# Modulation group 10: from four column products on TensorE to four row sums on VectorE

## The chip, the cores and the metric

The kernel runs on one core of a Trainium2 chip. Its time is the device time of one execution in microseconds (us), and a kernel's figure is the median over its runs. Five engines work in parallel, each through its own instructions in order: TensorE (PE, matrix products; PEld is its weight load), VectorE (DVE, elementwise arithmetic), ScalarE (ACT, activations, copies and casts), GpSimd (POOL, nearly unused here) and SyncE (SP), which issues nearly all DMA transfers from main memory (HBM) into the on-chip memory (SBUF). Products are collected in PSUM banks and taken from there by VectorE or ScalarE.

## The reference

One decoder layer over 256 tokens of width 2048, in float32. What matters here:

```python
mod = jax.nn.silu(c) @ w_ada[l] + b_ada[l]          # c: (1, 2048), w_ada: (2048, 12288)
shift_m, scale_m, gate_m, shift_f, scale_f, gate_f = jnp.split(mod[:, None, :], 6, axis=-1)
h = rms_norm(x, norm_mix_g[l]) * (1.0 + scale_m) + shift_m
proj = h @ w_in[l]                                   # attention heads | Mamba-2 heads
mix = jnp.concatenate([attn, ssm], axis=-1) @ w_out[l]
x = x + gate_m * mix
h = rms_norm(x, norm_ffn_g[l]) * (1.0 + scale_f) + shift_f
x = x + gate_f * conv_ffn(h, w_up[l], ...)           # then a last RMSNorm
```

`mod` is a vector of 12,288 numbers made from one vector `c`; its weights are 96 MB, 96 blocks of 128 outputs. Blocks 40 to 43 are part of `gate_m`, with which the output projection is scaled.

## The kernel before, in words

**Matrix products.** A large product (`w_in`, `w_out`, `w_up`, `w_down`) comes in units of 1 MB. A unit is loaded by SP into a staging buffer (`load_unit`, L250), split by `hi_lo_part` (L255) into a rounded half `h_...` (cast on ACT, L258) and a remainder `l_...` (subtraction on DVE, L259), 1024 columns at a time, and then multiplied by `mm3` (L276 to L279): three products for each block, two with the rounded half and one with the remainder. So no unit's products can all run before DVE has made its remainders. From the step `open` to the step `close2` there are three staging buffers, used in turn by the units of the large products and of the modulation alike: the load of a unit waits until the unit three before it has been used up.

**The modulation.** The 96 blocks of `mod` are 24 groups of four, and each group is four 1 MB units. There are two ways of working a unit, and the set `ON_PE` (L39) says for each group which one (`ada_unit`, L206). A group in `ON_PE`: a unit holds four of the 16 slices of the long axis for all four blocks, and PE multiplies each slice with its part of silu(c) (L217), four products of 32 columns that go to four quarters of one PSUM bank; after the fourth unit ACT copies the bank (`row`, L221), four one-column products turn it into columns (`adc`, L224) and DVE copies these into `mod` (L227). A group not in `ON_PE`: a unit holds one block, transposed, and a single DVE instruction multiplies it with silu(c) along the free axis and sums it up into one column of `mod` (L210), 2048 elements in each of 128 rows, followed by the read of its accumulator. The layout of `w_ada` is made on the host for either way; the bytes are the same.

**The order.** The first part of the kernel (projection, attention, state-space heads, output projection) follows a list written by hand, `ORDER` (L70). Its names: `ada.g.i` is unit i of modulation group g; Q, B, Z, V are units of the input projection; S0, S1, S2 are the stages of an attention head; `an`, `cb` and `dt` prepare the norm and the state-space heads; T1, T2, N, NG are the stages of these heads; O.0.i and O.1.i are units of the output projection. Around group 10 it reads:

```python
S1.5 S2.3 S0.7 ada.10.0 S2.4 ada.10.1 Q4.3 S1.6 dt S1.7 S2.5 ada.10.2 B3.1 ada.10.3 B3.2 ada.11.0 ada.11.1 S2.6
Z3.0 CS.0.8 S2.7 an ada.11.2 CS.8.12 Z3.1 cb.0 cb.1 ZS T1.0 T1.1 ada.11.3 O.0.0 ada.12.0 T2.0 T1.2 N.0 T2.1
```

From this list a planner with a cost model of its own makes one fixed instruction order for each engine; some steps (`HPS`, L32, the head stages among them) get a higher priority there. An instruction whose input is late holds up all that stand behind it on its engine.

**The steps that matter here.** B3.0, B3.1, B3.2 end with a convolution of each result (`conv_pair`, L359): DVE adds up `u` (L398), ACT starts the sum (L365), and DVE adds three shifted terms to it (L367). Z3.1 is the last unit of the input projection; DVE adds its result into `sz` (L388), and then ACT takes silu of `sz` (L373, step ZS) and of `cxs` (L370, CS.8.12). T1.0, the first state-space step, starts on PE with the transpose `xt` of `cxs` (L533). The gate from group 10 is first read at L638, ahead of the first output unit's scaling.

Of the kernel before, what the change touches and what calls it, by code (L numbers as in the profile page):

```python
# [35 lines left out]
          + [[32 + 4 * g + i for i in range(4)] for g in range(4)]  # L36
          + [[48 + 2 * g, 64 + 2 * g, 49 + 2 * g, 65 + 2 * g] for g in range(8)]
          + [[80 + 4 * g + i for i in range(4)] for g in range(4)])
ON_PE = {0, 6, 9, 10, 11, 12, 13, 14, 16}  # L39

HEADS = [(h, 8 + h) for h in range(8)]
XS = [(24 + 2 * i, 25 + 2 * i) for i in range(4)]
# [52 lines left out]
def hymba_layer(ctx, tc, xT, c_row, cT, w_ada, vecs, consts, relb, onehot, w_vdt, w_in, w_out, w_up1, w_up, w_dn, outT):  # L95
# [103 lines left out]
    def ada_load(g, i):  # L199
        ws = ws_tile(f"ada{g}_{i}")  # L200
        nc.sync.dma_start(ws[:, :D], w_ada[4 * g + i])
        return ws
# [3 lines left out]
    def ada_unit(g, i):  # L206
        ws = ada_pre.pop((g, i)) if (g, i) in ada_pre else ada_load(g, i)
        if g not in ON_PE:
            j = GROUPS[g][i]
# [458 lines left out]
    def ada_step(g, i):  # L668
        ada_unit(g, i)
        if g < 8:  # L670
            if g in ON_PE:
                if i == 3:
# [198 lines left out]
def _layout(a):  # L871
# [22 lines left out]
    for g, t in enumerate(GROUPS):  # L894
        for i in range(4):
            if g in ON_PE:
                ada.append(np.stack([wa[4 * i:4 * i + 4, :, c, :] for c in t], axis=2)
# [37 lines left out]
```

## Time and profile before

| | us |
|---|---|
| median of 3 runs | 1192.63 (1192.25 to 1193.84) |
| the profiled execution | 1191.71 |
| its span, first to last instruction | 1189.9 |
| busy: PE, PEld, DVE, ACT | 1162.5, 1112.3, 914.0, 637.7 |

The profile is one execution, and all positions below are us from the start of its span. The span is 1.81 us shorter than that execution's device time, and that execution was 0.92 us shorter than the median. A row of the timeline gives start, duration, engine, line, operation, output and inputs, shape and count, and in brackets the idle time before it with what ended it. The group of work around `ada.10` lies between 258 and 303, of the whole hand-ordered part (0 to about 460).

### The profile page before, as it was taken

Reading aid. Unit: us, or ns where it says so; the run is one execution under the profiler, and the core shown is the slowest. Engines: PE = TensorE matmul, PEld = TensorE weight load, DVE = VectorE, ACT = ScalarE, POOL = GpSimd, SP = SyncE. Lnnn points to the kernel's source line nnn. Section 1 sums busy time; section 2 is a strip of 40 time slices with the busy share of each in tenths; the row PEclk is TensorE's granted clock in tenths of the full one; section 3 lists DMA queues with packets and bytes.
Section 4 is the critical chain, followed back from the end, with each engine's and each line's share of the span. In section 5 each row is a group of like instructions: output and inputs, shape, how many; then the busy total and the mean of one; then the engine's idle time right before and its main releaser. Section 6 shows DMA issues by size and latency. Waiting matters only on the chain.

```text
span 1189.9 us, 23403 instructions
## 1 busy us (share of the span) xinstructions
PE 1162.5 (98%) x9760; PEld 1112.3 (93%) x9760; DVE 914.0 (77%) x1380; ACT 637.7 (54%) x959; POOL 0.9 (0%) x7
## 2 busy tenths in 40 slices
PE   7899999999999999999999999999999999999996
PEld 3899999988888898999999999999999999999995
DVE  3999969977988899786699974446898888655554
ACT  5545434357786545545576754444555555555552
POOL 0000000000000000000000000000000000000000
PEclk8899999999999999999999999999999999999998
DMA  9989898777766997987555435558878776545552
GB/s 369 414 307 360 322 346 313 252 277 254 284 245 215 367 384 292 366 318 288 201 190 196 162 116 192 193 193 283 298 288 313 285 279 218 202 147 195 195 195 96
DMA packets 47444, 309.60 MB, mean 260 GB/s; under 512 B 5568, under 2 KB 6761, under 8 KB 16105
## 3 DMA queue, kind: packets, MB, share of 16 engines
q1 hardware_dynamic: 46170, 307.04, 70.3%
q10 hardware_dynamic: 1168, 1.06, 0.5%
q8 instruction: 76, 1.25, 0.4%
q14 instruction: 30, 0.25, 0.1%
HBM read 305.98 MB, written 2.11 MB: 259 GB/s over the span
## 4 chain that ended last, share of the span: by engine, by line
PE 86%; DVE 6%; DMA 5%; ACT 1%; issue 1%; SPq 0%; DVEq 0%; ACTq 0%
PE ua L279 7%; PE da L278 7%; PE da L277 7%; PE ua L278 7%; PE da L279 7%; PE ua L277 7%; PE u1a L277 3%; PE u2a L278 3%; PE u1a L278 3%; PE u2a L277 3%; PE wa L277 3%; PE u1a L279 3%; PE u2a L279 3%; PE va L348 3%; PE wa L279 3%; PE wa L278 3%
## 5 line engine op out<-in xcount | busy, mean ns | idle before, releaser
L258 ACT CAST h_u<-s_u 128x1024 fp32r<-128x1024 f32 x176 | 184.8, 1051 | 196.6 <-PE ua L278 94.6
L259 DVE TENSOR_TENSOR l_u<-s_u,h_u 128x1024 fp32r<-128x1024 f32 x176 | 214.2, 1222 | 65.1 <-ACT h_u L258 64.6
L277 PE MATMUL ua<-h,h_u 128*128 128x256 f32 x704 | 194.3, 276 | 0.0
L278 PE MATMUL ua<-h,h_u 128*128 128x256 f32 x704 | 194.3, 276 | 0.0
L279 PE MATMUL ua<-h,l_u 128*128 128x256 f32 x704 | 194.3, 276 | 0.0
L279 PE MATMUL da<-g,l_d 128*128 128x256 f32 x704 | 194.3, 276 | 0.0
L278 PE MATMUL da<-g,h_d 128*128 128x256 f32 x704 | 194.3, 276 | 0.0
L277 PE MATMUL da<-g,h_d 128*128 128x256 f32 x704 | 194.1, 276 | 0.0
L259 DVE TENSOR_TENSOR l_d<-s_d,h_d 128x1024 fp32r<-128x1024 f32 (+1 forms) x128 | 108.8, 887 | 83.6 <-ACT h_d L258 83.6
L277 PE MATMUL wa<-hT,h_w 128*128 128x256 f32 x576 | 163.9, 285 | 4.6 <-ACT h_w L258 3.5
L278 PE MATMUL wa<-hT,h_w 128*128 128x256 f32 x576 | 161.0, 280 | 0.0
L279 PE MATMUL wa<-hT,l_w 128*128 128x256 f32 x576 | 160.1, 280 | 0.4 <-DVE l_w L259 0.4
L258 ACT CAST h_d<-s_d 128x1024 fp32r<-128x1024 f32 (+1 forms) x128 | 98.2, 782 | 114.9 <-PE da L278 106.8
L210 DVE SCALAR_TENSOR_TENSOR ada<-ada,cb 128x2048 f32<-128x2048 f32 x60 | 136.9, 2284 | 11.0 <-DMA ada<-w_ada 10.9
L278 PEld LDWEIGHTS da<-g,h_d 128*128 128x128 f32 x704 | 132.1, 188 | 0.0
L277 PEld LDWEIGHTS ua<-h,h_u 128*128 128x128 f32 x704 | 132.1, 188 | 0.0
L278 PEld LDWEIGHTS ua<-h,h_u 128*128 128x128 f32 x704 | 132.1, 188 | 0.0
L279 PEld LDWEIGHTS ua<-h,l_u 128*128 128x128 f32 x704 | 132.1, 188 | 0.0
L279 PEld LDWEIGHTS da<-g,l_d 128*128 128x128 f32 x704 | 132.1, 188 | 0.0
L277 PEld LDWEIGHTS da<-g,h_d 128*128 128x128 f32 x704 | 132.1, 188 | 0.0
L277 PEld LDWEIGHTS wa<-hT,h_w 128*128 128x128 f32 x576 | 109.4, 190 | 12.9 <-ACT h_w L258 4.6
L258 ACT CAST h_w<-s_w 128x1024 fp32r<-128x1024 f32 x72 | 73.7, 1048 | 88.9 <-PE wa L278 47.3
(237 smaller groups left out, 2676.9 us busy)
## 6 DMA issues: line engine op xcount, KB each, us to landing
ada<-w_ada SPq DMA_DIRECT2D x96, 1024.0 KB, 6.9
s_u<-w_up SPq DMA_DIRECT2D x88, 1024.0 KB, 5.0
s_d<-w_dn SPq DMA_DIRECT2D x64, 704.0 KB, 4.0
s_w<-w_in SPq DMA_DIRECT2D x36, 1024.0 KB, 7.5
s_o<-w_out SPq DMA_DIRECT2D x16, 1024.0 KB, 6.5
s_v<-w_vdt SPq DMA_DIRECT2D x8, 1040.0 KB, 8.8
x<-xT SPq DMA_DIRECT2D x4, 512.0 KB, 4.8
outT<-x SPq DMA_DIRECT2D x2, 640.0 KB, 3.0
```

The costliest lines, as they stand in the source:

```text
L210: dve.scalar_tensor_tensor(ws[:, :D], ws[:, :D], 1.0, cb, op0=ALU.mult, op1=ALU.mult, accum_out=mod[:, j:j + 1])
L258: act.copy(wh[:, :m], ws[:, o:o + m])
L259: dve.tensor_sub(wl[:, :m], ws[:, o:o + m], wh[:, :m].bitcast(F32))
L277: pe.matmul(o, whs, a[:, 0:T], start=first, stop=False)
L278: pe.matmul(o, whs, a[:, T:2 * T], start=False, stop=False)
L279: pe.matmul(o, wls, a[:, 0:T], start=False, stop=last)
L348: pe.matmul(va[tt][i][:, :n], lo if st == 1 else hi, (wl if st == 2 else wh)[:, s], start=f and st == 0, stop=l and st == 2)
```

## The change

Group 10 is taken out of `ON_PE`. Its four units stay at their places in `ORDER` and are loaded as before, in the other layout. The four groups of products (L217), the copy on ACT (L221), the one-column products (L224) and the copy into `mod` (L227) go; four instructions of L210, each with its accumulator read, come. One PSUM tile of the tag `ada` and one of `aux` fewer are handed out.

```diff
-ON_PE = {0, 6, 9, 10, 11, 12, 13, 14, 16}
+ON_PE = {0, 6, 9, 11, 12, 13, 14, 16}
```

## Rows read from the trace of the kernel before

**Rows 1.** Busy time by stretch: PE, PEld, DVE, ACT, POOL, clock, DMA share, GB/s.

```profile
120.00:140.00 20.00, 20.00 (x179) 20.00 (x178) 20.00 (x28) 7.85 (x9) 0.00 (x0) 1.00 0.91 336
262.00:277.10 15.10, 15.10 (x118) 12.92 (x117) 6.90 (x15) 9.62 (x25) 0.00 (x0) 1.00 0.74 267
277.10:328.70 51.60, 51.60 (x411) 43.00 (x410) 47.08 (x99) 40.50 (x82) 0.00 (x0) 1.00 0.74 277
332.50:402.50 70.00, 69.83 (x556) 57.92 (x556) 59.81 (x125) 47.58 (x95) 0.00 (x0) 1.00 0.65 238
```

**Rows 2.** Chain of waits, 270 to 302: start, time on the chain, what.

```profile
270.23 0.99 PE adp L217 x6
...
278.96 1.83 PE adp L217 x10
...
289.23 0.99 PE adp L217 x8
...
294.48 0.99 PE adp L217 x8
295.47 0.32 PE wa L279
295.79 0.12 PE wa L277
...
300.91 0.12 PE adc L224 x2
...
301.41 0.56 PE adc L224 x6
```

**Rows 3.** Timeline of DVE, 30 to 33: one unit of a row group.

```profile
30.23 2.28 DVE L210 SCALAR_TENSOR_TENSOR ada<-ada,cb 128x2048 f32<-128x2048 f32 x1
32.44 0.08 DVE L210 DVE_READ_ACCUMULATOR ada<-ada,cb 128x1 f32 x1
```

**Rows 4.** Timeline of DVE, 271 to 320: holes, and the copy into `mod`.

```profile
274.38 0.69 DVE L398 TENSOR_TENSOR u<-cxs,wa 128x512 f32<-128x512 f32 x1 [2.40 <-PE wa L279]
277.11 1.23 DVE L259 TENSOR_TENSOR l_w<-s_w,h_w 128x1024 fp32r<-128x1024 f32 x1 [2.05 <-ACT h_w L258]
...
299.33 1.37 DVE L367 SCALAR_TENSOR_TENSOR cxs<-u,vec,cxs 128x255 f32<-128x255 f32 x3 [0.76 <-ACT cxs L365]
...
302.53 0.16 DVE L227 COPY mod<-adc 128x4 f32<-128x4 f32 x1
...
311.01 1.37 DVE L367 SCALAR_TENSOR_TENSOR cxs<-u,vec,cxs 128x255 f32<-128x255 f32 x3 [0.67 <-ACT cxs L365]
```

**Rows 5.** Timeline of SP's queue: loads of `ada.10.0` and `10.1`, `10.2`, B3.1, `10.3`.

```profile
258.91 8.51 SPq L201 DMA_DIRECT2D ada<-w_ada  x2
...
279.96 0.33 SPq L201 DMA_DIRECT2D ada<-w_ada  x1
280.38 0.38 SPq L252 DMA_DIRECT2D s_w<-w_in  x1
280.86 0.38 SPq L201 DMA_DIRECT2D ada<-w_ada  x1
```

**Rows 6.** Chain of waits, 308 to 333.

```profile
308.40 6.82 DMA s_w<-w_in
...
319.05 1.75 DVE rs_attn L300
...
328.72 0.80 ACT sz L373
...
330.55 1.90 ACT cxs L370
...
332.50 0.44 PE xt L533 x2
```

**Rows 7.** Landing of the `ada` load issued at 258.91, and of all issued from 255 to 300.

```profile
ada<-w_ada SPq DMA_DIRECT2D x1, 1024.0 KB, 9.3
...
DMA to landing us min/median/max: 4.8/6.8/9.3
```

## The prediction

> **What bounds the kernel now.** Read the busy times by stretch first [rows 1]. From 262 to 328.7 PE is busy in every microsecond, with no idle time the profile shows, at a granted clock of 1.00. DVE stands at 6.90 of 15.10 us up to 277.1, and then at 47.08 of 51.60 us: 91%, with 4.52 us of holes. After the first state-space step has started, from 332.5 to 402.5, PE is at 69.83 of 70.00 us and DVE at 59.81, so 10.19 us of DVE are free there. PE is the engine without room over the whole part, but from 277.1 to 328.7 DVE is nearly as full, and PE can't do a unit before DVE has made its remainders.
>
> Then the chain of waits. Around group 10 it runs through PE, the group's own products among it [rows 2]. From 308.40 to 332.50 it does not: it goes over the load of the input projection's last unit, a cast, then through DVE from 319.05 to 328.72, through the two silu of ACT, and comes back to PE with the transpose `xt` at 332.50 [rows 6]. So in that stretch PE works beside the chain, and what it does there is cover.
>
> Third, who holds the staging buffers [rows 5]. The loads of `ada.10.0` and `ada.10.1` are issued from 258.91 on, but that of `ada.10.2` only at 279.96 and B3.1's at 280.38. The three products of `ada.10.0` that PE took at 270.23 left the fourth for 278.96 [rows 2], and the buffer was held so long.
>
> **What goes from PE.** Four pieces of the chain are the group's products: 0.99, 1.83, 0.99 and 0.99 us, together 4.80 [rows 2]. The second holds ten records because it has the rest of unit 0 and all of unit 1. The first ordinary product behind a piece shows 0.32 us where the next shows 0.12, so entering and leaving costs 0.20 a piece, 0.80 for four. The one-column products are 0.12 + 0.56 = 0.68. In all 4.80 + 0.80 + 0.68 = 6.28 us of PE. If PE were the only limit this would be the gain, 1191.71 - 6.28 = 1185.4 by the profiled execution. The copies on ACT and DVE go too; DVE's is 0.16 [rows 4], of which about 0.12 separates it from the next instruction by my estimate from the 0.07 by which an accumulator read overlaps its neighbour [rows 3].
>
> **What comes to DVE.** One unit is 2.28 us, with the accumulator's read it ends 2.29 us after its start, and the read begins after 2.21 [rows 3]. Next to other work I count 2.21, alone in a hole 2.29. Four are 8.84 us, less 0.12 for the copy.
>
> Where they fall is set by when their data land. `ada.10.0` lands 9.3 us after 258.91, at 268.2. `ada.10.1` is the second of the two issues in a row that ends at 267.42; one issue is 0.33, so it goes out at 267.09, and with the 6.8 us median of this stretch it lands at about 273.9 [rows 5, 7]. DVE has a hole of 2.40 us up to 274.38 and one of 2.05 up to 277.11, waiting first for PE and then for ACT [rows 4]. The first takes unit 0 whole, at no cost. The second takes 2.05 of unit 1's 2.29: 0.24 are left over. If the planner puts neither there, both go behind 277.1 and cost up to 4.42.
>
> Units 2 and 3 land later than 280 in any order near this one and fall into the full stretch: 2 x 2.21 = 4.42 us against 4.52 us of holes. Not every hole can be filled. Three of them are the wait for ACT between `u` and the convolution's first term, of which 0.76 and 0.67 are the first and the last and the middle one is 0.67 too: 2.10 us [rows 4]. They are a round trip from DVE to ACT and back, and are made again however late DVE runs, unless other work stands behind them in the order. I take 4.52 - 2.10 = 2.42 as what a late DVE can take back. So DVE comes to the end of the stretch late by 0.24 + 4.42 - 2.42 - 0.12 = 2.12 us. The bounds from both sides: if every hole of both stretches can be used, 8.20 + 4.52 = 12.72 against 8.72 of new work, DVE ends 4.0 us early; if none can, 8.72 late. I take 2.1: two units in holes long enough for them, two in a stretch whose longest hole is a third of one unit.
>
> **What that does to the end.** DVE's last addition into `sz` ends the DVE piece at 328.72, and both silu and the transpose follow without slack [rows 6], so the first state-space step starts 2.1 us later, at 334.6. PE's 6.28 us don't help there: PE comes to this place earlier, and waits, since the next units of the output projection need remainders from the same DVE and buffers that DVE frees. From 332.5 on PE has 70 us of its own work without gaps [rows 1], none of it changed, and DVE's 10.19 free us keep DVE out of the way. So the lateness is carried to the end: 1191.71 + 2.1 = 1193.8 for an execution like the profiled one, and beside the median, 0.92 above it, 1192.63 + 2.1 = 1194.7. I forecast 1194.7.
>
> The earlier release of buffers is costed at nothing. With unit 0 done by 274.4 the load of `ada.10.2` could go out 5.6 us sooner, and B3.1's with it. That is real, but it brings casts and remainders that the same full DVE has to make. If the cover is DVE's fullness and it is gone, this release is what lets PE's gain through; that is the first rival.
>
> At one place a rule speaks on this. PE's busy time is 51.60 of 51.60 us in the full stretch, PEld's is 43.00 and DVE's 47.08 [rows 1]. The Trainium skill (Perfetto Trace Analysis, "Identifying the Most-Contended Engine") says that the busy time of matrix products is a poor measure of how close TensorE is to its limit, and that its weight loads are to be read instead, while for VectorE occupancy is a fair one. By that rule TensorE has 8.60 us of room there and VectorE 4.52, so VectorE is the more contended, and the 6.28 us would bring nothing; by PE's own column it would be 1185.4. The pieces [rows 2] favour neither alone, as the group's products load few weights for the time they take.
>
> **The rivals.**
>
> *PE's time comes through.* Here DVE keeps up and the chain follows PE. For it: from 120 to 140 DVE is busy 20.00 of 20.00 us while PE has 179 products and no gap [rows 1], so a full DVE need not stop PE; the holes before 277.1 are 8.20 us; and loads go out sooner. Against it: the chain's DVE piece. The gain is bounded by DVE's 4.0 us at the start of the state-space step, and by 6.28 on PE if that step's lateness is absorbed by the 10.19 us behind it. I take 4: 1188.6.
>
> *PE waits for remainders.* One mechanism: the planner sets a 2.2 us row sum ahead of the remainders of B3.1, B3.2 or Z3.0, and PE, in order, stops for them, without the group's products that stood there as filling. The place is PE's change to a new unit, three of them between 280 and 310. It decides as soon as two of the four sums stand there; a sum costs its 2.21, and with all four and the lost holes the price is the upper bound, 8.7. With three it is 6.6: 1199.2. Against it: the remainders can be taken first, as the sums' results are first needed at L638, after 340.
>
> *Nothing is seen.* The lateness is lost in the 10.19 us of DVE and in PE's filling behind 332.5, or the planner moves both by like amounts. Then 1192.6. For it: PE's work after 332.5 is what sets the end, and some output units could be pulled ahead of the first state-space step.
>
> That the change doesn't do what it says can be left out: the same list chooses path and layout.
>
> **How the numbers follow.** Chances: the forecast, DVE a little late, 0.40; PE's time comes through 0.31; PE waits for remainders 0.15; nothing is seen 0.14. About 0.2% is what a measurement of this kernel can tell from no change, here 2.4 us: 1190.2 to 1195.0. The forecast itself lies close inside that bound; it runs from 0 to 5 late, and I count 0.15 of it as same and 0.25 as slower. With the second rival slower is 0.40. The first rival is faster but for 0.02 of it, 0.29. The rest, 0.15 + 0.14 + 0.02, is 0.31 for same. The range goes from 1187.6, a gain of 5, to 1199.5, just over the second rival with three sums; outside lie PE's full gain and the bound of 8.7. Cases of both signs hold much of the chance; the forecast's own range is 1192.6 to 1197.6.
>
> **What would show it.** In the profile after, DVE from 262 to 330 should show four rows of L210, two of them where the holes of 2.40 and 2.05 were; DVE in what was 277.1 to 328.7 should be above 95%; `xt` should start some 2 us later, and PE should show idle time or weight-load waits just ahead of it, ended by ACT or DVE. From `xt` to the end the distance should be as before, 857 us. Wrong would be: `xt` earlier by 3 us or more with PE still without gaps (the first rival), PE idle at remainders between 280 and 310 (the second), or a distance from `xt` to the end that changes by over 2 us, which would put the effect into the state-space part, where I have none.

## The result and the profile after

The changed kernel takes 1204.70 us (median of 4 runs, 1204.04 to 1205.60), the kernel before 1192.44 us in the same comparison (1191.36 to 1193.84): a ratio of 1.0099, 95% interval 1.0087 to 1.0111. It is slower by 12.3 us, where the prediction had 2.1, and outside its range. In the experiments below the kernel before came to 1192.1 to 1193.2 us.

The profiled execution after took 1204.94 us, its span 1203.2; before it was 1191.71 and 1189.9. So the spans differ by 13.3 us, and five distances add up to it:

| distance | before | after | difference |
|---|---|---|---|
| start of the span to `xt` of T1.0 | 332.50 | 340.78 | +8.28 |
| `xt` to the sum of squares `ssg` of step NG.1 (L623) | 63.38 | 62.48 | -0.90 |
| `ssg` to the first product of O.1.0 (`oa<-cats`) | 6.76 | 10.19 | +3.43 |
| O.1.0 to `ssx` (L604), the end of the output projection | 48.76 | 52.28 | +3.52 |
| `ssx` to the end | 738.50 | 737.47 | -1.03 |

First the busy time by stretch of the changed kernel (columns as in [rows 1]):

```profile
262.00:277.10 15.10, 15.10 (x121) 13.77 (x120) 11.05 (x19) 7.97 (x19) 0.00 (x0) 1.00 0.89 326
277.10:328.70 51.60, 47.39 (x355) 38.86 (x355) 48.72 (x96) 37.36 (x81) 0.00 (x0) 1.00 0.81 294
332.50:402.50 70.00, 70.00 (x558) 58.26 (x560) 54.63 (x119) 46.75 (x89) 0.00 (x0) 1.00 0.54 196
400.00:420.00 20.00, 10.05 (x58) 7.78 (x57) 12.58 (x21) 8.89 (x14) 0.00 (x0) 0.67 0.80 319
```

and the last of these stretches in the kernel before:

```profile
400.00:420.00 20.00, 18.54 (x158) 15.73 (x157) 17.30 (x25) 11.93 (x19) 0.00 (x0) 1.00 1.02 420
```

PE, without a gap before, has 4.21 us of gaps from 277 to 329. DVE does 4.15 us more up to 277.1 and only 1.64 more behind it [rows 1]. And there is a place that the prediction doesn't speak of: from 400 to 420 PE has 58 rows where it had 158, at a granted clock of 0.67. The timeline of PE shows both places; in brackets is the idle time ahead of a row and what ended it:

```profile
290.70 0.70 PE L441 MATMUL s<-qk 128*128 128x256 f32 x2 [0.63 <-DVE qk L382]
...
302.39 1.06 PE L217 MATMUL adp<-ada,c 128*32 128x512 f32 x8 [1.00 <-DMA ada<-w_ada]
...
307.39 0.70 PE L467 MATMUL o<-pts,vdt 128*128 128x256 f32 x2 [0.64 <-ACT pts L465]
...
312.33 0.38 PE L277 MATMUL wa<-hT,h_w 128*128 128x256 f32 x1 [1.11 <-DVE u L398]
...
338.74 1.07 PE L217 MATMUL adp<-ada,c 128*32 128x512 f32 x8
339.73 0.39 PE L277 MATMUL oa<-cat,h_o 128*128 128x256 f32 x1
...
340.78 0.38 PE L533 MATMUL xt<-con,cxs 128*128 128x128 f32 x2
...
403.26 0.70 PE L623 MATMUL ssg<-sqa,ones 128*128 128x256 f32 x2
...
413.45 0.58 PE L277 MATMUL oa<-cats,h_o 128*128 128x256 f32 x1 [9.49 <-ACT h_o L258]
413.83 0.41 PE L278 MATMUL oa<-cats,h_o 128*128 128x256 f32 x1
```

Between 277 and 329 five short waits stand, each for another engine's work (the fifth, at 310.30, is 0.66, behind `pts` like the third); no remainder is among their releasers. From 312.33 to `xt` at 340.78 PE has no gap at all. At 413.45 PE has waited 9.49 us, a place at which the kernel before still had work:

```profile
395.88 0.59 PE L623 MATMUL ssg<-sqa,ones 128*128 128x256 f32 x2
...
400.41 1.92 PE L217 MATMUL adp<-ada,c 128*32 128x512 f32 x16
402.64 0.39 PE L277 MATMUL oa<-cats,h_o 128*128 128x256 f32 x1 [0.31 <-ACT h_o L258]
```

The four sums themselves cost what they should, in the timeline of DVE (as [rows 3]):

```profile
268.22 2.29 DVE L210 SCALAR_TENSOR_TENSOR ada<-ada,cb 128x2048 f32<-128x2048 f32 x1 [0.43 <-DMA ada<-w_ada]
...
272.84 2.28 DVE L210 SCALAR_TENSOR_TENSOR ada<-ada,cb 128x2048 f32<-128x2048 f32 x1
...
279.78 2.29 DVE L210 SCALAR_TENSOR_TENSOR ada<-ada,cb 128x2048 f32<-128x2048 f32 x1
...
287.76 2.27 DVE L210 SCALAR_TENSOR_TENSOR ada<-ada,cb 128x2048 f32<-128x2048 f32 x1
```

What stands ahead of `xt` is another row than before. There the last `u` was made at 315.40, and the path to `xt` went over `sz` and its silu [rows 6]. Now the last `u` comes 11.3 us later, and its convolution and the last silu stand behind rounding and remainders of the output projection's first units. The timelines of DVE and of ACT:

```profile
326.70 0.68 DVE L398 TENSOR_TENSOR u<-cxs,wa 128x512 f32<-128x512 f32 x1
...
331.14 1.23 DVE L259 TENSOR_TENSOR l_o<-s_o,h_o 128x1024 fp32r<-128x1024 f32 x1 [1.32 <-ACT h_o L258]
332.29 2.45 DVE L367 SCALAR_TENSOR_TENSOR cxs<-u,vec,cxs 128x255 f32<-128x255 f32 x6
```

```profile
331.01 1.09 ACT L365 ACTIVATE cxs<-u,vec 128x256 f32<-128x256 f32 x2
...
333.42 1.92 ACT L373 ACTIVATE sz<-sz 128x2048 f32<-128x2048 f32 x1
335.25 1.98 ACT L258 CAST h_o<-s_o 128x1024 fp32r<-128x1024 f32 x2
337.13 1.91 ACT L370 ACTIVATE cxs<-cxs 128x2048 f32<-128x2048 f32 x1
```

The silu of `cxs` ends at 339.04, where it ended at 332.45 [rows 6]: 6.6 of the 8.28 us. The other 1.74 us are PE's own queue. Counted in the trace, PE has 104 products of the output projection ahead of `xt` where it had 48, and it is still busy with these when `cxs` is ready.

The second place, by the chain of waits:

```profile
403.33 0.64 PE ssg L623 x2
403.99 8.28 DMA s_o<-w_out
412.35 1.05 ACT h_o L258
413.43 1.24 DVE l_o L259
414.71 0.58 PE oa L279
415.29 0.21 PE oa L277
```

O.1.0's load is issued just behind `ssg`, at 403.99. In the kernel before it is so as well, at 396.51, and no other load goes out in the 4.8 us ahead of it. Now SP issues one of `ada.14.3` at 402.53 and O.1.3's at 403.39, and while these are landing O.1.0's takes 8.28 us for 1 MB. SP's queue before and after (a row of x3 merges three loads, and in both the second of the three is O.1.0's):

```profile
391.72 5.59 SPq L252 DMA_DIRECT2D s_o<-w_out  x3
```

```profile
402.53 0.33 SPq L201 DMA_DIRECT2D ada<-w_ada  x1
403.39 1.41 SPq L252 DMA_DIRECT2D s_o<-w_out  x3
```

### The profile page after: what moved, and what is told of

It reads as the page before. It is cut to its first block, busy times and chain, and to the rows that moved or that the text cites. A ratio compares the mean times of both kernels' runs of the same rounds, so it can differ in the third digit from the quotient of the medians.

```text
span 1203.2 us, 23323 instructions
## 1 busy us (share of the span) xinstructions
PE 1162.3 (97%) x9720; PEld 1113.4 (93%) x9720; DVE 921.2 (77%) x1387; ACT 636.4 (53%) x957; POOL 0.9 (0%) x7
## 4 chain that ended last, share of the span: by engine, by line
PE 89%; DVE 5%; DMA 3%; ACT 2%; issue 1%; SPq 0%; DVEq 0%; ACTq 0%
PE ua L279 7%; PE ua L278 7%; PE da L279 7%; PE da L278 7%; PE da L277 7%; PE ua L277 7%; PE wa L277 4%; PE wa L279 4%; PE wa L278 4%; PE va L348 4%; PE u2a L277 3%; PE u1a L277 3%; PE u1a L278 3%; PE u1a L279 3%; PE u2a L279 3%; PE u2a L278 3%
## 5 line engine op out<-in xcount | busy, mean ns | idle before, releaser
L210 DVE SCALAR_TENSOR_TENSOR ada<-ada,cb 128x2048 f32<-128x2048 f32 x64 | 146.2, 2287 | 24.2 <-DMA ada<-w_ada 24.2
```

Of the source, the lines that this page charges most:

```text
L210: dve.scalar_tensor_tensor(ws[:, :D], ws[:, :D], 1.0, cb, op0=ALU.mult, op1=ALU.mult, accum_out=mod[:, j:j + 1])
```

## The experiments

`xt` is given as its distance from one addition on DVE (L308, at 261.89 before, 261.79 after), ahead of which no sum or product of the group has run; up to there the executions differ by as much as 3.4 us. That distance is 70.6 us before and 79.0 after.

| kernel | median, us | ratio to before (95%) | addition to `xt` | idle PE ahead of O.1.0 |
|---|---|---|---|---|
| after | 1204.70 | 1.0099 (1.0087 to 1.0111) | 79.0 | 9.49 |
| e1_short | 1200.05 | 1.0061 (1.0046 to 1.0076) | 70.4 | 9.48 |
| e2_both | 1203.55 | 1.0094 (1.0079 to 1.0109) | 80.7 | 0 |
| e3_u2 | 1205.06 | 1.0112 (1.0094 to 1.0130) | 76.8 | 2.79 |
| e4_oldfirst | 1199.61 | 1.0050 (1.0035 to 1.0065) | 81.2 | 0 |
| e5_before_oldfirst | 1198.47 | 1.0055 (1.0040 to 1.0070) | 71.5 | 0 |
| e7_first | 1202.24 | 1.0085 (1.0070 to 1.0100) | 80.2 | 6.01 |
| e8_short_first | 1195.48 | 1.0023 (1.0013 to 1.0032) | 69.7 | 6.10 |
| e9_g13_first | 1198.83 | 1.0054 (1.0039 to 1.0069) | 71.2 | 5.97 |
| e6_half | 1206.87 | 1.0110 (1.0092 to 1.0127) | 77.6 | 10.43 |
| e10_first_two | 1203.29 | 1.0084 (1.0066 to 1.0103) | 81.6 | 9.45 |
| e11_last_two | 1199.50 | 1.0051 (1.0034 to 1.0068) | 79.8 | 2.24 |
| e12_fill | 1191.91 | 0.9990 (0.9980 to 1.0000) | 70.0 | 1.50 |
| e13_full_order8 | 1199.82 | 1.0071 (1.0056 to 1.0087) | 74.0 | 5.94 |
| e14_short_order | 1204.31 | 1.0106 (1.0089 to 1.0123) | 79.7 | 9.51 |
| e15_full_order12 | 1195.83 | 1.0027 (1.0016 to 1.0037) | 73.3 | below 0.1 |

The distance to `xt` holds one thing beside sums and order. In six profiled executions the granted clock falls to its lower level for a few us on this stretch; in the other eleven, those of the kernel before and of the changed kernel among them, it does not. From the mean granted clock I estimate that this is 1.7 us of the distance in e3, e4, e10 and e14, and 3.4 us in e2 and e11.

The last column is 0.31 in the kernel before. In e4 and e5 PE waits later instead, 3.07 us at 410.78 and 2.6 us at 411.96, within the same half of the output projection.

### Which side of the change costs

**e1_short**, the changed kernel with sums of 32 columns, the rest of each left out:

```diff
-            dve.scalar_tensor_tensor(ws[:, :D], ws[:, :D], 1.0, cb, op0=ALU.mult, op1=ALU.mult,
+            n = 32 if g == 10 else D
+            dve.scalar_tensor_tensor(ws[:, :n], ws[:, :n], 1.0, cb[:, :n], op0=ALU.mult, op1=ALU.mult,
```

> The changed kernel, but each of group 10's four row sums takes 32 of its 2048 columns, so that DVE has nearly nothing to do for the group; loads, places in the order and the missing products on PE are as in the changed kernel. Theory A (DVE's 8.8 us of sums delay the convolutions of B3 and with them the first state-space step): the step's transpose starts at 333 or sooner and the time is 1184 to 1192 us. Rival B (not the sums but what the missing products leave behind: buffers freed at other times, no filling on PE, another order): the time stays at 1200 us or more.

The lateness of `xt` is gone: 70.4, as before. The time is still 7.4 us above the kernel before, although PE has 6.28 us less to do by the prediction's sum and DVE nearly nothing more. PE starts O.0.0 earlier, 58.2 us behind the addition instead of 62.4, and then waits 9.48 us for O.1.0. From `xt` to `ssg` it takes 65.94 us instead of 63.38, and what was PE's filling behind `ssg` now stands ahead of it. So there are two separate losses, and the second does not need the length of the sums.

**e2_both**, the kernel before with its products kept, and DVE products beside them whose result nobody reads:

```diff
+        if g == 10:
+            for k in range(8):
+                s = slice(192 * k, 192 * k + 192)
+                dve.tensor_mul(dump, ws[:, s], cb[:, s])
```

> The kernel before, with its products of group 10 on PE, and on top of them eight DVE products of 192 columns for each of the group's four units, some 2.2 us a unit, whose result is not used. Theory A: DVE is late as in the changed kernel and the time is 1200 to 1212 us. Rival B: DVE's time is hidden, 1190 to 1195 us.

1203.55, and `xt` at 80.7, of which 3.4 are the lower clock. The added DVE work makes `xt` late with PE's products in place too, in the order that the planner makes for it; length and order are not taken apart here. O.1.0 doesn't wait: PE has its filling.

### What was suspected first

**e3_u2**: a second `u` buffer, paid for with one of `pts`, since in the changed kernel the last `u` waits until the convolution ahead of it is done.

```diff
-                u = mtmp(f"u{i}", 512, "u", 1)
+                u = mtmp(f"u{i}", 512, "u", 2)
-        pts = mtmp(f"pts{h}", 384, "pts", 2)
+        pts = mtmp(f"pts{h}", 384, "pts", 1)
```

> The changed kernel with two buffers for the convolution's input u in place of one (paid for by one buffer for pts in place of two). Theory A in its narrow form (the convolutions queue behind the single u): the last u moves from 326.7 to 320 or sooner, the transpose from 340.8 to 336 or sooner, 1196 to 1201 us. If the row of u is only late because DVE as a whole is: 1203 to 1206 us.

The last `u` moves from 326.70 to 317.25, and the time stays: 1205.06. The one buffer isn't the cause, as far as this shows; what the buffer of `pts` costs that was given up for it was not tried by itself.

**e4_oldfirst**, after with the three old staging buffers first in turn behind `close2`, and **e5_before_oldfirst**, the same in the kernel before:

```diff
         wst["pat"] = [0, 0, 0, 1, 1, 1]
+        wst["i"] = 0
```

> The changed kernel, but the loads after close2 take the three old staging buffers first and the three new ones after them, so that the load of O.1.0 need not wait for the norm product ssg of the last state-space group. Theory C (PE's idle time of 9.5 us before O.1.0, and the half clock behind it, come from that load being issued late and behind two others): the idle time falls below 5 us, the clock stays up, 1193 to 1199 us. If the state-space heads' lateness is what holds O.1.0, by the data themselves: 1202 to 1206 us.

> The kernel before, with the loads after close2 taking the three old staging buffers first, so that O.1.0's load need not wait for ssg. Theory: before the change this wait was covered by products of O.0.7, PE idle 1.46 us in all there, so 1190.5 to 1193 us; if O.1.1 and ada.14.2, now last, come late: 1194 to 1199.

With an old buffer O.1.0's load doesn't wait for `ssg`, and the changed kernel gains 5.1 us, while `xt` stays as late as it was. The same line makes the kernel before 5.6 us slower, as now O.1.1 is late there. What helps one order hurts another.

### The order of the loads

**e7_first** and **e8_short_first**: the loads of `ada.14.3` and O.1.3 are issued behind O.1.1's, so that O.1.0's goes out first; e7 has full sums, e8 those of 32 columns.

```diff
-        nc.sync.dma_start(ws[:, :n], src)
+        if name == "o1_3":
+            with tc.issue_after(box["o1_1"].ins):
+                nc.sync.dma_start(ws[:, :n], src)
+        else:
+            box[name] = nc.sync.dma_start(ws[:, :n], src)
...
+        if (g, i) == (14, 3):
+            with tc.issue_after(box["o1_1"].ins):
```

> The changed kernel with one thing put back to what it was before the change: the loads of ada.14.3 and O.1.3 go out behind those of O.1.0, O.1.1 and ada.14.2, not ahead of them. Theory C (O.1.0's load goes out 0.7 us later than it could and then shares the DMA engines with the two loads ahead of it, 8.3 us to landing against some 5): O.1.0's first product comes 6.5 to 7.5 us after ssg, not 10.2, PE's idle time falls from 9.5 to about 6, and the time is 1199 to 1201.5 us. If the order of the loads has no part in it: 1203.5 to 1206.

> Sums of 32 columns as in the first experiment, and the loads around O.1.0 in the order of before as well: what is left of the change is the missing products on PE and the earlier release of buffers. Theory C: 1200.05 less 3.4 for the load and up to 1.5 for a shorter idle time, 1194 to 1197, still above the kernel before, since PE has spent its filling by the time the state-space heads end. If PE's 6.3 us are worth something once DVE and the loads are out of the way: below 1192.

The chain of waits in e7:

```profile
404.82 4.80 DMA s_o<-w_out
```

The load takes 4.80 us instead of 8.28 (4.89 in e8), O.1.0 comes 6.7 and 6.8 us behind `ssg`, 6.76 in the kernel before, and the time falls by 2.5 us with full sums and by 4.6 with short ones. Six us of idle PE are left in both, here by the timeline of PE in e8:

```profile
397.29 0.70 PE L632 MATMUL ssg<-sqa,ones 128*128 128x256 f32 x2
...
404.09 0.58 PE L286 MATMUL oa<-cats,h_o 128*128 128x256 f32 x1 [6.10 <-ACT h_o L267]
```

In the kernel before PE had 34 products of O.0.7 and those of two modulation units (the sixteen rows above, two for each product) to do behind `ssg` and waited 0.31 us. In e8 all of them come ahead of it.

### A place where DVE has room

**e9_g13_first**: group 10 back on PE, group 13 as rows instead. Its sums stand in the stretch where DVE has 10.19 us free [rows 1]. The load order is that of e7.

```diff
-ON_PE = {0, 6, 9, 10, 11, 12, 13, 14, 16}
+ON_PE = {0, 6, 9, 10, 11, 12, 14, 16}
```

> The kernel before with group 13, and not 10, as rows on DVE (its places lie between 356 and 387, where DVE had 10 us free), and the loads around O.1.0 in the order of before. Theory A, DVE's fullness at the place decides: the first state-space transpose stays at 332.5 and the time is 1190 to 1196 us. If any group taken from PE costs about the same wherever its sums are: 1199 us or more.

`xt` is not late, but `ssg` comes 68.8 us behind it instead of 63.4, and PE, nearly without gaps in this stretch before, gets 4.5 us of them. This is the busy time from 332.5 to 402.5 in e9:

```profile
332.50:402.50 70.00, 65.50 (x516) 55.67 (x514) 64.68 (x124) 45.52 (x89) 0.00 (x0) 0.99 0.58 211
```

DVE's free time in a stretch did not say whether sums can be put there at no cost. How much of this is the planner's other order was not tried for group 13.

### Is it DVE's time?

Three doses, in the changed kernel: **e6_half**, four sums of 1024 columns, the rest left out; **e10_first_two**, units 0 and 1 full, 2 and 3 with 32 columns; **e11_last_two**, the other way round.

```diff
+            n = 1024 if g == 10 else D                          # e6
+            n = 32 if g == 10 and i in (2, 3) else D            # e10
+            n = 32 if g == 10 and i in (0, 1) else D            # e11
```

> The changed kernel with all four sums over 1024 of the 2048 columns (half of each sum is left out), so that each takes about half its time, at the same four places. If the cost is DVE's time, it is proportional: xt at 337 and 1202 us, halfway between 1200.05 (32 columns) and 1204.7 (2048). If holes take back a fixed amount, as the prediction has it, half the work costs far less than half: xt at 333 to 334 and 1200 us.

> The changed kernel; of group 10's four sums, those of units 0 and 1 run over all 2048 columns and those of units 2 and 3 over 32 columns (the rest of these two sums is left out). The order of the loads is the changed kernel's, so O.1.0's load still stands behind two others. Theory of the prediction (the first two sums fall into DVE's holes and cost nothing): as with all four sums short, xt at 333 and 1200 us. Theory now (each sum pushes what stands behind it, wherever it stands): xt at 336 to 338, about 1202 us.

> The changed kernel; the sums of units 2 and 3 run over all 2048 columns, those of units 0 and 1 over 32 columns (the rest of these two sums is left out). O.1.0's load stands ahead of ada.14.3's and O.1.3's here, as in the kernel before, so about 3 us are to be taken off the time for that. Theory of the prediction (these two carry the whole cost): xt at 340, as with all four. Theory now: xt halfway, 336 to 338; time 1198 to 1200 us.

e6 and e10 fit neither of their theories; e11's `xt` is where the prediction's theory has it, its time where the later one does. Half the work, the first two or the last two make `xt` about as late (77.6, 81.6, 79.8; without the lower clock 77.6, 79.9, 76.4) as all of it (79.0). So the lateness doesn't go with DVE's time, as the later theory had it, and the kernel with the first two sums alone is not spared, as the prediction's theory had it. What differs between these kernels besides the sums is the planner's order of their instructions. Against the changed kernel, e1 has 207 of the 607 DVE instructions of the first part at another place in their engine's order, e6 167, e10 183 and e11 222; on PE it is 494 to 763 of 3105.

### Length against order

This was still open, so the order was taken out of the planner's hands. At the end of the first part each instruction is tied behind its predecessor in a written list, on PE, DVE, ACT and SP; the list is the order that the planner had made for another kernel. On PE and DVE the tied kernels have as many instructions as the changed kernel (9720 and 1387).

```diff
+    for eng, text in FIXED.items():
+        ids = sorted(place[eng])
+        prev = None
+        for run in text.split():
+            a, b = (int(v) for v in (run.split("-") * 2)[:2])
+            for n in ids[bisect_left(ids, a):bisect_right(ids, b)]:
+                if prev is not None:
+                    tc.add_manual_dep(place[eng][n], prev, ...)
+                prev = place[eng][n].name
```

**e13_full_order8** has full sums in the order of e8, **e14_short_order** has short sums in the order of the changed kernel.

> The changed kernel with its four full sums, every engine's instructions of the first part in the order that the planner made for the kernel with sums of 32 columns and O.1.0's load ahead (1195.48 us, xt at 331.34). Only the length of the four sums differs from that kernel. Theory A (the sums' 8.8 us of DVE push the chain): xt at 338 to 339 and about 1203 us. Theory B (what costs is the other order that the planner makes when it has the full sums to place): xt at 333 to 335, 1196 to 1199 us.

> The changed kernel with sums over 32 of 2048 columns (the rest is left out), every engine's instructions of the first part in the order that the planner made for the changed kernel with its full sums. Only the length of the sums differs from the changed kernel (1204.7 us, xt at 340.78). Theory A (DVE's time): the lateness goes, xt at 333 and about 1200 us, as with the planner's own order for short sums. Theory B (the order): xt stays at 337 to 340 and the time at 1202 to 1204 us although DVE has nearly no sums to make.

e14 decides for the order. Its sums take 0.19 us each, at the places of the changed kernel's, and `xt` (79.7) and the time are about those of the changed kernel. First its DVE, then its PE:

```profile
268.28 0.19 DVE L282 SCALAR_TENSOR_TENSOR ada<-ada,cb 128x32 f32<-128x32 f32 x1 [0.49 <-DMA ada<-w_ada]
...
286.27 0.18 DVE L282 SCALAR_TENSOR_TENSOR ada<-ada,cb 128x32 f32<-128x32 f32 x1
...
327.59 0.68 DVE L470 TENSOR_TENSOR u<-cxs,wa 128x512 f32<-128x512 f32 x1
```

```profile
341.48 0.38 PE L605 MATMUL xt<-con,cxs 128*128 128x128 f32 x2
...
414.16 0.58 PE L349 MATMUL oa<-cats,h_o 128*128 128x256 f32 x1 [9.51 <-ACT h_o L330]
```

That `xt` is even a little later than in the changed kernel goes with the clock. PE's gaps ahead of 312 are nearly the same in both executions, but only in e14 does the granted clock fall behind them. The changed kernel's stretch first, then e14's, and below it e14's busy time in the full stretch:

```profile
312.00:320.00 8.00, 7.67 (x58) 6.55 (x59) 7.77 (x15) 5.18 (x9) 0.00 (x0) 1.00 0.72 245
```

```profile
312.00:320.00 8.00, 8.00 (x51) 6.88 (x49) 6.33 (x12) 4.51 (x7) 0.00 (x0) 0.79 0.48 188
277.10:328.70 51.60, 47.55 (x349) 39.38 (x349) 44.32 (x92) 37.09 (x79) 0.00 (x0) 0.97 0.77 290
```

Without its 1.7 us e14 would stand at 78.0 by this estimate: 7.6 us behind e1, which has the same short sums in its own order, and 1.0 ahead of the changed kernel. So the order is most of the lateness, and not quite all of it. Whether the other executions of e14 had this fall of the clock too isn't known, as one was profiled; if so, the length of the sums is worth up to 2.1 us of the time here and not 0.4.

e13 lies between its two theories. In a kept order the full sums make `xt` 4.3 us later than in e8 (74.0 against 69.7), and the time 4.3 us longer. So the sums are not free when nothing is moved. At `xt` that is about half of what the other order costs; in the time the two weigh alike, since from e1 to e14, the same short sums in the two orders, it is 4.3 us as well: in e14 more of PE's work is already done when `xt` comes.

### PE's saved time

**e12_fill**: e8 with half of O.0.7's products and those of `ada.14.0` and `ada.14.1` behind `ssg` instead of ahead of it.

```diff
-O.0.7 ada.14.0 N.7 ada.14.1 NG.1 close2
+N.7 NG.1 O.0.7 ada.14.0 ada.14.1 close2
...
+            with (tc.issue_after(box["ssg"].ins) if fill and w == 1 else ExitStack()):
...
+        with (tc.issue_after(box["ssg"].ins) if g == 14 and i < 2 else ExitStack()):
```

> The changed kernel with the sums over 32 columns and O.1.0's load put ahead (1195.48 us so far, with 6.1 us of idle PE ahead of O.1.0), and beside that PE's order written so that half of O.0.7's products and those of ada.14.0 and ada.14.1 come behind the sum of squares ssg instead of ahead of it. Theory: PE's saved time was lost because nothing was left to fill the wait from ssg to O.1.0; with that filling kept, the idle time falls to about 2 us, ssg comes at 394 to 395, O.1.0 at about 401, and the time is 1191 to 1193.5 us. Rival: the distance to O.1.0 is set by something else; ssg no earlier, 1195 us or more.

The timeline of PE in e12:

```profile
394.52 0.70 PE L634 MATMUL ssg<-sqa,ones 128*128 128x256 f32 x2 [1.62 <-DVE sqa L628]
...
401.40 0.39 PE L287 MATMUL oa<-cats,h_o 128*128 128x256 f32 x1 [1.50 <-ACT h_o L268]
```

1191.91 us, 3.6 less than e8: `ssg` comes 2.8 us earlier, and the wait ahead of O.1.0 falls from 6.10 to 1.50. Against the kernel before it is 1.3 us less, at the edge of its interval. That is the most that PE's 6.28 us brought in any kernel here, with DVE nearly free of sums and load order and filling put in their favour. The kernel before was not given the same list, so the 1.3 us may be in part the list's. **e15_full_order12** has full sums in the whole order of e12:

> Full sums again, in the order of the kernel that keeps PE's filling behind ssg (1191.91 us with sums of 32 columns). Theory A: xt 7 us later than there, about 1199 us. Theory B: 1192 to 1196 us, so no slower than the kernel before by more than 0.2%, and group 10 as rows would then cost nothing once the order is kept.

1195.83 us, the fastest kernel here with group 10 as rows in full, and still 0.27% (0.16 to 0.37) slower than the kernel before. That is in the time of theory B, but `xt` is 3.3 us later than in e12 and the time 3.9 longer, so the sums do cost something in this order too.

## Why the prediction was wrong

The times make a ladder from the changed kernel down, one thing undone at each step:

| kernel | sums | order of the first part | O.1.0's load | filling behind `ssg` | us | step |
|---|---|---|---|---|---|---|
| after | full | made for full sums | behind two others | no | 1204.70 | |
| e7 | full | made for full sums | first | no | 1202.24 | 2.5 |
| e13 | full | made for short sums | first | no | 1199.82 | 2.4 |
| e15 | full | made for short sums | first | yes | 1195.83 | 4.0 |
| e12 | 32 columns | made for short sums | first | yes | 1191.91 | 3.9 |

The intervals of after and e7, and of e7 and e13, overlap, so the two upper steps are of the size of what can be told apart; the lower two are not in doubt. By the ratios, each taken against the kernel before beside it, the steps come to about 1.7, 1.7, 5.2 and 4.4. Another sequence would share the sum out otherwise: in the changed kernel's own order the length of the sums is worth 0.4 (e14, or up to 2.1 without the lower clock), in e8's 4.3 (e13).

**What goes from PE** was right in what came of it and not in the reason: nothing of the 6.28 us came through in the change, and at most 1.3 did in e12. But PE does not come to `xt` early and wait there, as forecast. It has no gap from 312.33 on and does 56 more products of the output projection ahead of `xt`, which are then missing as filling behind `ssg`. The Trainium skill (Perfetto Trace Analysis, "Identifying the Most-Contended Engine") takes occupancy as a fair measure of how close VectorE is to its limit. By the prediction's rows VectorE was the more contended. The traces agree that nothing came through, and not on the reason: in e14 VectorE is busy for 44.32 us from 277.1 to 328.7, less than before [rows 1], and the kernel is as slow as the changed one. Neither engine's busy time told what the change would cost.

**What comes to DVE** is the step that failed. Its durations were right: four of 2.27 to 2.29 us against 2.28. What failed is the balance of work and holes, in two ways. It put the sums into the holes of the old trace, which supposes that everything around them stays in its order. The planner made another order: the first sum starts at 268.22, ahead of the hole of [rows 4], and the last `u`, at 315.40 before, comes at 326.70. `xt` was 8.4 us later by the distance above where 2.1 was forecast, and e14 shows that the order does most of that with sums of 0.19 us. And in an order kept fixed the term was too small as well: 4.3 (e13 against e8) and 3.3 (e15 against e12) of lateness. Between short and full the four sums differ by 8.4 us, so 4.1 and 5.1 went into holes, where the prediction had 6.6 of its 8.72. Which of its holes failed, the two for the first sums or the 2.42 us, no run separates.

**What that does to the end** failed in its second half. The lateness went to the end of the state-space heads nearly unchanged, as forecast (62.48 from `xt` to `ssg`, 63.38 before), with PE at 70.00 of 70.00. That was in part luck, as PE's work there did change: the products pulled ahead of `xt` are gone from it, and the filling from behind `ssg` has come in (in e1 the distance is 65.94). And "none of it changed" left out what stands behind 402.5. PE now comes to `ssg` with its filling done and waits for a load that had been covered, and that load stands behind two others in SP's queue: 3.43 us, and 3.52 more behind the wait, most of it at the lower clock. The prediction asks for PE's cover ahead of `xt` and not there. The sign that it named for this case, a distance from `xt` to the end changed by over 2 us, was seen: 862.4 against 857.4. Of its other signs, idle time of PE just ahead of `xt` was not seen, and DVE came to 94% of the full stretch and not above 95%.

**The rivals.** "PE waits for remainders" came nearest in size (8.7 at most, where `xt` is 8.4 late) and had the wrong mechanism. PE does get 4.04 us of idle time from 290 to 313, but behind `qk`, a load, `pts` twice and `u`, and with sums of 0.19 us at the same places (e14) the time is no better. "PE's time comes through" and "nothing is seen" were wrong, with 12.3 us of loss; what the latter was argued from, output units pulled ahead of the first state-space step, did happen, and did not help. That the earlier release of buffers costs nothing wasn't tried by itself.

**What stays open** is which exchange within the planner's order costs the 7.6 to 9.3 us at `xt` (e14 against e1). The last convolution and silu behind the output projection's casts, and PE's output products ahead of `xt`, are what the trace shows last; e3 moved the last `u` forward and gained nothing, and no run exchanged single instructions.

## What to carry to other kernels

A cost that is laid into the holes of an old trace holds at best for a fixed order, and here not even there. Where a planner remakes the order, take the change's length away and keep the order (e14) before believing that the engine's time is the cost. Where an engine is relieved, ask what its work had covered further on: here the first long wait behind the place is where the gain was lost, and filling put there gave part of it back (e12). And look at the queue of loads: here two loads issued ahead held up the one that was needed next.

## What was not expected of the hardware

After 9.49 us of idle time PE's products came at a step of 0.21 us, from 413.45 to 420.21, at a granted clock of 0.50, where the kernel before shows 0.11 at a granted clock of 1.00: the lower of the two levels, 1.2 instead of 2.4 GHz. These are 27 products. Without the one wait among them they took 6.3 us; the first 27 of the kernel before, without theirs, took 3.4. So 2.9 us, most of the 3.52 by which the distance from O.1.0 to `ssx` grew, are the clock's. Here the wait cost once more behind it.

A 1 MB load landed in 8.28 us with two others issued 1.46 and 0.60 us ahead of it, and in 4.80 us where it went first (e7).
